# Four more input projections of layer 0 as 512-column products, with an order for minima, copies and sums

## The chip, the cores and the metric

The kernel runs on one core of one Trainium2 chip. The metric is device time in microseconds (us): the median of several executions of the whole program. Before the change it is 244.56 us (three runs, 244.37 to 244.6).

## What is computed

The reference is a decoder trunk of two layers on x of shape 1 x 256 x 1024 (256 positions, model width 1024, all float32). Each layer normalises x, projects it once to 3584 columns, feeds three branches side by side, and projects their gated outputs back:

```
hn   = rms_norm(x, norm_gain)
proj = hn @ w_in                      # 1024 -> 3584 columns
a_q, a_k, a_v, a_g, b_x, b_g, c_q, c_k, c_v, c_g = split(proj)
y_a = dilated_attention(rope(a_q), rope(a_k), a_v) * silu(a_g)   # 8 heads of 64
y_b = rg_lru(b_x) * silu(b_g)                                    # width 256
y_c = stick_breaking(c_q, c_k, c_v) * silu(c_g)                  # 4 heads of 64
x   = x + concat(y_a, y_b, y_c) @ w_out
```

A final `rms_norm` follows the second layer. The dilated attention adds up three windows of dilation 1, 4 and 16 under one softmax. The recurrent branch is a causal convolution of width 4, two sigmoid gates and a linear recurrence h = a h + u. Stick-breaking attention weighs keys by running products of sigmoids.

## The kernel before

**Split products.** Float32 accuracy comes from splitting each operand into a rounded high part (type float32r) and the remainder, the low part, and adding three products: high by high, high by low and low by high. For the activations, `xx` holds both parts side by side: `xh = xx[:, :, 0]`, `xl = xx[:, :, 1]`, eight blocks (k) of 128 features, each 256 positions wide. For the weights, `load_chunk` (L102) brings a chunk of 256 output columns (2048 values on each of 128 partitions) in two transfers of 1024 columns through five staging buffers `st`. For each 512 columns ACT writes the high part (`whi`, L115), and DVE subtracts it from the staged values for the low part (`wlo`, L117). A staging buffer can be loaded again when its two subtractions are done. Chunks are asked for one or two ahead of their use, and four sets of `whi` and `wlo` exist.

**Two forms of projection.** `proj_b` (L326) computes one chunk transposed: 256 output columns in two halves b of 128, each for all 256 positions. The plain form runs 24 products of 256 columns a half (L225, through `mm3`), all three terms into one accumulator; both halves share one PSUM bank, and the reader takes its result from PSUM. The paired form (the chunk is in `PAIRED[l]`) multiplies each high weight block by `xh` and `xl` at once, 512 columns wide (L344, 8 products), and the low weight block by `xh`, 256 wide (L341, 8 products). A half then fills a whole bank: the left 256 columns hold two terms, the right 256 hold high by low. ACT copies the right part into `low` (L347, two buffers) and DVE adds the left part to it (L349). There are three PSUM banks for all projections (pool `pp`), four for scores and transposes (`at`), one for weighted values (`yp`).

**Layer 0 and its scale.** In layer 0 the projections run on x times the gain without the normalisation: the factor 1/rms of each position is multiplied in afterwards, as a row vector `rb` broadcast over partitions. `scaled` (L410) does so in one DVE operation that reads PSUM, `rotated` (L503) does it in the rotation (with a table already multiplied by `rb`) and for the unrotated features (L518). In layer 1, x is normalised first and no factor is needed.

**Order of a layer.** The chunks come in this order: stick-breaking q, k; first dilated q, k (heads 0 to 3); recurrent input (`CH_BX`); second dilated q, k (`CH_AQ[1]`, `CH_AK[1]`, heads 4 to 7); stick-breaking gate (`CH_CG`); recurrent gate (`CH_BG`); two chunks of dilated gate (`CH_AG`, `CH_AG + 1`); four chunks of the output projection (`CH_O` on). Between the two halves of some chunks other work of PE is placed (`mid`): between those of the second q, the scores of heads 0 to 3 (L542), after which DVE takes minima of the masked scores (L549, which also write the shifted scores), ACT the exponentials with their sums (L84), DVE reciprocals and the division (L560, L562). Transposes of these weights (L489) stand between the stick-breaking gate and the recurrent gate; between the halves of the recurrent gate come the gates' products (L601), weighted values (L453) and the scores of heads 4 to 7. After the recurrent gate, `lru_scan` computes the recurrence, and `emit_y` (L437) multiplies it by its gate and splits it into `yh` (L441) and `yl` (L442), which the output projection reads.

**What sets the order.** PE's instructions run in the order in which the program writes them. Those of ACT, DVE and POOL are put in order beforehand by a planner that takes the earliest written instruction that its own estimate of times holds ready; each engine then works through its fixed list and waits where an input or a buffer isn't ready. `dep` (L63) adds an edge to the planner: one instruction comes after another on the same engine's list, without a wait on the chip. Transfers of weights are issued by the SP queue in program order, each when its staging buffer is free.

Layer 0 before pairs only the two chunks of dilated gate, layer 1 all its chunks of `proj_b`.

## Time and profile before

| what | value |
|---|---|
| median of 3 runs | 244.56 us (244.37 to 244.6) |
| profiled execution: its own time, its span | 246.06 us, 244.2 us |
| PE, matmuls busy | 236.2 us (97%), 1651 |
| PE, weight loads busy | 206.6 us (85%), 1651 |
| DVE busy | 200.0 us (82%), 480 |
| ACT busy | 174.4 us (71%), 384 |
| granted TensorE clock | 0.999 |
| DMA | 43.89 MB, mean 180 GB/s |

The span runs from the first to the last instruction on the core; the execution's own time has some 1.9 us around it. PE's busy time counts overlapping products once. The chain of waits follows the work that ended last back to the start; its pieces, in order of time, show where PE runs without a hole. A row of a timeline gives start, length, engine, line, operation, output and inputs, shape and count of neighbours that were merged, and in brackets the idle time of the engine just before and what ended it.

### The profile page before, as it was taken

What the parts mean: (1) busy time and instruction counts of PE and PEld (TensorE: products, weight loads), DVE (VectorE), ACT (ScalarE), POOL (GpSimd) and SP (SyncE); (2) the same over time, 40 slices, a digit from 0 to 9 for tenths busy, and PEclk for the clock granted to TensorE, in tenths of its full rate; (3) what the DMA queues carried; (4) which work ended last, traced back from release to release, by engine and by line L of the source; (5) the groups of instructions that cost most, each with busy time, mean ns of one, the idle gap of its engine ahead of it and who ended that gap; (6) DMA issues with size and microseconds to landing.
All of it is one profiled execution on the core that took longest, in us unless ns stands there. A gap on an engine that the chain in (4) does not pass through costs nothing.

```text
span 244.2 us, 4576 instructions
## 1 busy us (share of the span) xinstructions
PE 236.2 (97%) x1651; PEld 206.6 (85%) x1651; DVE 200.0 (82%) x480; ACT 174.4 (71%) x384; POOL 10.5 (4%) x43
## 2 busy tenths in 40 slices
PE   8799999999999999999999999999999999999991
PEld 4588999999999798878888888888888878887881
DVE  3694699999999889999495585999999986997362
ACT  3677987919597689994673674876669867998143
POOL 0017200002000000000000000000010000000000
PEclk9999999999999999999999999999999999999999
DMA  6989988565846843068448288615470771000022
GB/s 193 377 254 390 384 268 291 190 205 177 240 152 207 272 153 105 1 195 320 175 134 273 88 289 268 199 44 177 171 214 7 226 282 63 31 0 0 3 75 97
DMA packets 14037, 43.89 MB, mean 180 GB/s; under 512 B 1728, under 2 KB 3008, under 8 KB 14016
## 3 DMA queue, kind: packets, MB, share of 16 engines
q1 hardware_dynamic: 13248, 42.43, 51.9%
q0 software_dynamic: 192, 0.52, 0.8%
q10 hardware_dynamic: 576, 0.66, 0.7%
q8 instruction: 13, 0.21, 0.4%
q14 instruction: 8, 0.07, 0.1%
HBM read 42.03 MB, written 1.05 MB: 176 GB/s over the span
## 4 chain that ended last, share of the span: by engine, by line
PE 94%; DMA 3%; DVE 1%; SPq 0%; ACT 0%; issue 0%; DVEq 0%
PE pp L225 34%; PE pp L344 20%; PE pp L341 10%; PE s L225 9%; PE s L181 4%; PE s L489 3%; DMA st<-first 3%; PE y L453 2%; PE pp L383 2%; PE s L542 2%; PE pp L181 2%; PE s L469 1%; PE y L225 1%; PE pp L453 1%; PE s L601 1%; PE s L273 1%
## 5 line engine op out<-in xcount | busy, mean ns | idle before, releaser
L117 DVE TENSOR_TENSOR wlo<-st,whi 128x512 fp32r<-128x512 f32 x128 | 81.8, 684 | 7.5 <-ACT whi L115 6.9
L115 ACT ACTIVATE whi<-st 128x512 fp32r<-128x512 f32 x130 | 72.5, 627 | 9.0 <-DMA st<-w_pack 3.4
L344 PE MATMUL pp<-xx,whi 128*128 128x512 f32 x208 | 50.8, 393 | 0.0
L344 PEld LDWEIGHTS pp<-xx,whi 128*128 128x128 f32 x208 | 37.8, 188 | 7.6 <-DVE q L349 0.3
L225 PE MATMUL pp<-xx,whi 128*128 128x256 f32 x288 | 38.2, 285 | 0.0
L225 PEld LDWEIGHTS pp<-xx,whi 128*128 128x128 f32 x288 | 35.8, 191 | 0.8 <-issue 0.3
L341 PEld LDWEIGHTS pp<-xx,wlo 128*128 128x128 f32 x208 | 26.9, 191 | 1.6 <-ACT scr L84 0.3
L341 PE MATMUL pp<-xx,wlo 128*128 128x256 f32 x208 | 28.0, 284 | 0.0
L225 PE MATMUL pp<-xx,wlo 128*128 128x256 f32 x144 | 20.2, 283 | 0.0
L84 ACT ACTIVATE pr<-scr,mn 128x128 f32<-128x128 f32 (+1 forms) x32 | 14.1, 443 | 6.6 <-DVE mn L549 6.6
L225 PEld LDWEIGHTS pp<-xx,wlo 128*128 128x128 f32 x144 | 18.6, 192 | 0.0
L78 ACT ACT_TABLE_LOAD x13 | 16.7, 1283 | 1.9 <-PEq L847 1.7
L347 ACT ACTIVATE low<-pp 128x256 f32<-128x256 f32 x26 | 9.4, 373 | 8.8 <-PE pp L344 8.0
L225 PE MATMUL pp<-whi,yh 128*128 128x512 f32 (+1 forms) x48 | 14.1, 382 | 0.0
L225 PE MATMUL pp<-wlo,yh 128*128 128x512 f32 (+1 forms) x48 | 13.7, 372 | 0.0
L225 PE MATMUL pp<-whi,yl 128*128 128x512 f32 (+1 forms) x48 | 13.6, 371 | 0.0
L181 PE MATMUL s<-whi,xx 128*128 128x512 f32 (+1 forms) x36 | 9.6, 384 | 1.8 <-ACT xx L161 1.7
L225 PEld LDWEIGHTS pp<-whi,yl 128*128 128x128 f32 x48 | 8.6, 188 | 1.6
L225 PEld LDWEIGHTS pp<-wlo,yh 128*128 128x128 f32 x48 | 8.6, 188 | 1.6
L225 PEld LDWEIGHTS pp<-whi,yh 128*128 128x128 f32 x48 | 8.3, 188 | 1.6 <-issue 0.3
L549 DVE CUSTOM_DVE_ANT_0 scr<-s,con 128x128 f32<-128x128 f32 (+1 forms) x32 | 9.2, 350 | 0.0
L181 PEld LDWEIGHTS s<-whi,xx 128*128 128x128 f32 x36 | 6.0, 197 | 3.3 <-ACT xx L161 2.5
(189 smaller groups left out, 372.3 us busy)
## 6 DMA issues: line engine op xcount, KB each, us to landing
st<-w_pack SPq DMA_DIRECT2D x66, 512.0 KB, 5.3
st<-first SPq DMA_DIRECT2D x7, 512.0 KB, 7.0
xres<-x_in SPq DMA_DIRECT2D x4, 256.0 KB, 7.5
gw_t<-gate_w SPq DMA_DIRECT2D x2, 256.0 KB, 6.8
gn<-gains SPq DMA_DIRECT2D x2, 256.0 KB, 5.9
xs<-xc POOLq DMA_DIRECT2D x4, 128.0 KB, 3.8
gf<-gains SPq DMA_DIRECT2D x2, 256.0 KB, 5.4
out<-st ACTq DMA_DIRECT2D x2, 192.0 KB, 2.0
```

Source lines behind the costliest of these rows:

```text
L78: load = act.preload_act_table_set(name)
L84: i = dep(act.activation(*a, **k), loaded["load"])
L115: split[l, c] = act.activation(h, part, AF.Copy)
L117: dve.tensor_sub(r, part, h.bitcast(F32))
L181: pe.matmul(ps[t][:, c0:c1], a[:, k, t * P:(t + 1) * P], b, start=k == 0 and all(m[0] is not ps for m in seq[:i]), stop=k == NK - 1 and al ...
L225: pe.matmul(ps, a(k), b(k), start=first and i == 0, stop=last and i == len(seq) - 1, skip_group_check=skip)
L341: pe.matmul(ps[:, 0:S], lo[:, k, cs], xh[:, k, :], start=i == 0, stop=i == len(seq) - 1, skip_group_check=True)
L344: pe.matmul(ps, hi[:, k, cs], xx[:, k].rearrange("p h t -> p (h t)"), start=i == 0, stop=i == len(seq) - 1, skip_group_check=True)
L347: act.activation(low, ps[:, S:2 * S], AF.Copy, scale=sc)
L453: pe.matmul(y[hr, p * 128 + o:p * 128 + 256], vt[:, s0, hs], wts[i][s0], start=s0 == 0, stop=s0 == 1)
L489: pe.transpose(tp[:, i * P:(i + 1) * P], tiles[h0 + h][:, j * P:(j + 1) * P], ident)
L549: dve.tensor_tensor_reduce(xs[:, cs], sps[h][:, cs], nmask[:, cs], -0.125, 3e38, ALU.add, ALU.min, mn[:, t:t + 1])
```

## The change

Layer 0 now computes four more chunks in the paired form: the recurrent input, the second dilated q and k, and the stick-breaking gate. The recurrent gate, which sits around the longest piece of other work, stays in the plain form, and so do the first four chunks. For the paired chunks, the factor `rb` is multiplied in after the sums: for the recurrent input in place in the padded input of the convolution, for the gate from its own tile in `silu`, for q and k in the rotation.

The rest is order in layer 0. The four subtractions for the gate's weights come after the last minimum of the scores of heads 0 to 3, and three of them also after the sum of the second half of the second q. The exponentials of the last two of those heads come after that half's copy, and their reciprocals after its sum. The subtractions for the weights of the last dilated gate chunk come after the multiplication of the stick-breaking gate by `rb`. Layer 1's operations are the same as before.

```diff
--- before.py
+++ after.py
@@ -43,7 +43,7 @@
 
 CH_AV, CH_CV, CH_CQ, CH_CK, CH_BX, CH_CG, CH_BG, CH_AG, CH_O = 0, 2, 3, 4, 7, 10, 11, 12, 14
 CH_AQ, CH_AK = (5, 8), (6, 9)
-PAIRED = ((CH_AG, CH_AG + 1), (CH_CQ, CH_CK, CH_AQ[0], CH_AK[0], CH_BX, CH_AQ[1], CH_AK[1], CH_CG, CH_BG, CH_AG, CH_AG + 1))
+PAIRED = ((CH_BX, CH_AQ[1], CH_AK[1], CH_CG, CH_AG, CH_AG + 1), (CH_CQ, CH_CK, CH_AQ[0], CH_AK[0], CH_BX, CH_AQ[1], CH_AK[1], CH_CG, CH_BG, CH_AG, CH_AG + 1))
 
 
 @with_exitstack
@@ -97,7 +97,7 @@
 
     xx, xh, xl = x_tile()
 
-    split, rounds = {}, {}
+    split, rounds, rests = {}, {}, {}
 
     def load_chunk(l, c):
         hi = wsp.tile([P, 2048], F32R, name="whi", tag="whi")
@@ -114,7 +114,7 @@
                     part = v2(part)
                 split[l, c] = act.activation(h, part, AF.Copy)
                 rounds.setdefault((l, c), []).append(split[l, c])
-                dve.tensor_sub(r, part, h.bitcast(F32))
+                rests.setdefault((l, c), []).append(dve.tensor_sub(r, part, h.bitcast(F32)))
         return beside or (hi, lo)
 
     order = [(l, c) for l in range(L) for c in range(NCH) if l > 0 or c > CH_CV]
@@ -344,9 +344,9 @@
                             pe.matmul(ps, hi[:, k, cs], xx[:, k].rearrange("p h t -> p (h t)"), start=i == 0,
                                       stop=i == len(seq) - 1, skip_group_check=True)
                     low = wk.tile([P, S], F32, name="low", tag="low", bufs=2)
-                    act.activation(low, ps[:, S:2 * S], AF.Copy, scale=sc)
+                    last["low"] = act.activation(low, ps[:, S:2 * S], AF.Copy, scale=sc)
                     if sc == 1.0:
-                        dve.tensor_add(to[b], ps[:, 0:S], low)
+                        last["sum"] = dve.tensor_add(to[b], ps[:, 0:S], low)
                     else:
                         dve.scalar_tensor_tensor(to[b], ps[:, 0:S], sc, low, ALU.mult, ALU.add)
                 else:
@@ -358,8 +358,10 @@
             return flat
 
         def proj_to(dst, c, mid=None, sc=1.0):
-            if l > 0 and c in PAIRED[l]:
+            if c in PAIRED[l]:
                 proj_b(c, mid, [dst[:, b, :] for b in range(2)], sc)
+                if l == 0:
+                    dve.tensor_mul(dst, dst, rb.rearrange("p (o t) -> p o t", o=1).broadcast_to([P, 2, S]))
             else:
                 scaled(dst, proj_b(c, mid), sc)
 
@@ -410,7 +412,7 @@
         def scaled(dst, ps, sc=1.0):
             if l == 0:
                 a, b = rows(ps)
-                dve.scalar_tensor_tensor(dst, a, sc, b, ALU.mult, ALU.mult)
+                last["scaled"] = dve.scalar_tensor_tensor(dst, a, sc, b, ALU.mult, ALU.mult)
             else:
                 act.activation(dst, v2(ps), AF.Copy, scale=sc)
 
@@ -425,12 +427,15 @@
         if l > 0:
             tables()
 
+        def home(tile_):
+            return [tile_[:, b, :] for b in range(2)] if l == 0 else None
+
         def silu(dst, ps):
             sg = v2(scr(512))
-            src = v2(ps)
+            src = dst if ps is None else v2(ps)
             if l == 0:
-                src = v2(scr(512))
-                scaled(src, ps)
+                ps, src = src, v2(scr(512))
+                scaled(src, ps.rearrange("p b t -> p (b t)"))
             tab(sg, src, AF.Sigmoid)
             dve.tensor_mul(dst, src, sg)
 
@@ -503,19 +508,20 @@
         def rotated(c, tiles, h0, tag, mid=None):
             dst = tiles[h0] = sb.tile([P, 2, S], F32, name=tag, tag=tag)
             tab_ = rp0 if l == 0 else rp
-            if l > 0:
-                src = scr(S)
-                proj_b(c, mid, [src, dst[:, 1, :]])
+            pair = c in PAIRED[l]
+            if pair:
+                src, high = scr(S), dst[:, 1, :]
+                proj_b(c, mid, [src, high])
             else:
                 ps = proj_b(c, mid)
-                src = ps[:, 0:S]
+                src, high = ps[:, 0:S], ps[:, S:2 * S]
             sh = scr(S)
             dve.stream_shuffle(sh, src, SHUF)
             dve.tensor_mul(dst[:, 0, :], src, tab_[:, 0, :])
             dve.tensor_mul(sh, sh, tab_[:, 1, :])
             dve.tensor_add(dst[:, 0, :], dst[:, 0, :], sh)
             if l == 0:
-                dve.tensor_mul(dst[:, 1, :], ps[:, S:2 * S], rb)
+                dve.tensor_mul(dst[:, 1, :], high, rb)
 
         qT, kT, exact = {}, {}, {}
         prob = {}
@@ -546,18 +552,20 @@
                 xs = scr(384)
                 mn = wk.tile([P, 2], F32, name="mn", tag="mn", bufs=4)
                 for t, cs in halves:
-                    dve.tensor_tensor_reduce(xs[:, cs], sps[h][:, cs], nmask[:, cs], -0.125, 3e38,
-                                             ALU.add, ALU.min, mn[:, t:t + 1])
+                    last["min"] = dve.tensor_tensor_reduce(xs[:, cs], sps[h][:, cs], nmask[:, cs], -0.125, 3e38,
+                                                           ALU.add, ALU.min, mn[:, t:t + 1])
                 shifted[h] = xs, mn
             return shifted
 
         def dil_softmax(shifted):
+            last["exps"], last["recs"] = [], []
             for h, (xs, mn) in shifted.items():
                 pr = wk.tile([P, 384], F32, name="pr", tag="pr", bufs=4)
                 den = wk.tile([P, 2], F32, name="den", tag="den", bufs=4)
                 for t, cs in halves:
-                    tab(pr[:, cs], xs[:, cs], AF.Exp, bias=mn[:, t:t + 1], scale=-1.0, accum_out=den[:, t:t + 1])
-                dve.reciprocal(den, den)
+                    last["exps"].append(tab(pr[:, cs], xs[:, cs], AF.Exp, bias=mn[:, t:t + 1], scale=-1.0,
+                                            accum_out=den[:, t:t + 1]))
+                last["recs"].append(dve.reciprocal(den, den))
                 for t, cs in halves:
                     dve.tensor_scalar(pr[:, cs], pr[:, cs], den[:, t:t + 1], None, ALU.mult)
                 prob[h] = pr
@@ -654,12 +662,20 @@
             dil_softmax(dil_scores(0))
 
         rotated(CH_AQ[1], qT, 4, "q1", second)
+        if l == 0:
+            for r in rests[l, CH_CG]:
+                dep(r, last["min"])
+            for r in last["exps"][4:]:
+                dep(r, last["low"])
+            for r in (*last["recs"][2:], *rests[l, CH_CG][1:]):
+                dep(r, last["sum"])
         rotated(CH_AK[1], kT, 4, "k1")
         split_qk(4, ("q0", "ag"))
         table(SIGM)
-        cg_ps = proj_b(CH_CG)
+        cg_ps = proj_b(CH_CG, None, home(cg))
         pts = dil_transposes(0)
         silu(cg, cg_ps)
+        cg_scaled = last.get("scaled")
 
 
         y_half(0)
@@ -670,7 +686,11 @@
             y_c["y"] = values(va, pts, 0, bank(pp, "pp"))
             y_c["s"] = dil_scores(4)
 
-        silu(bg, proj_b(CH_BG, third))
+        bg_ps = proj_b(CH_BG, third)
+        if l == 0:
+            for r in rests[l, CH_AG + 1]:
+                dep(r, cg_scaled)
+        silu(bg, bg_ps)
         y_half(1)
         table(LN_EXP)
         lru_scan()
```

## The prediction

> **What bounds the kernel now.** I read the page's engine shares and slices first, then the chain of waits in order of time.
>
> ```profile
> span 244.2 us, 4576 instructions
> PE 236.2 (97%) x1651; PEld 206.6 (85%) x1651; DVE 200.0 (82%) x480; ACT 174.4 (71%) x384; POOL 10.5 (4%) x43
> ...
> DVE  3694699999999889999495585999999986997362
> ```
>
> PE is busy for 97% of the span, so every stretch of time that PE gets rid of shortens the kernel, and every wait that it takes on lengthens it. DVE is the engine beside it to watch: from slice 6 to slice 19 (about 31 to 116 us) it is at eight tenths or more throughout. The chain says the same of the stretch in question, and it prices the two kinds of product:
>
> ```profile
> 32.71 5.75 PE pp L225 x48
> ...
> 55.88 2.87 PE pp L225 x24
> 58.75 1.37 PE s L542 x38
> 60.12 14.59 PE pp L225 x120
> 74.71 1.31 PE s L489 x12
> 76.02 2.86 PE pp L225 x24
> ...
> 90.83 3.65 PE pp L344 x16
> ...
> 98.24 2.73 PE s L225 x12
> ...
> 102.29 5.48 PE pp L225 x24
> ...
> 141.27 1.84 PE pp L344 x8
> ...
> 176.29 1.15 PE pp L341 x8
> 177.44 3.65 PE pp L344 x16
> 181.09 1.91 PE pp L341 x16
> 183.01 3.83 PE pp L344 x16
> ```
>
> The rows down to 102.29 are layer 0, the others layer 1 (start, length, what, count). In layer 0 PE goes from one piece to the next without a hole. The 120 products at 60.12 are five halves: second q's other half (to 63.0), second k (to 68.9) and the gate (to 74.7). The last row is one to remember: it is 0.18 us longer than its twin at 177.44.
>
> **The change part by part.** *The products.* A half of an unpaired chunk is 24 products of 256 columns: 5.75 / 48 = 119.8 ns each, 2.875 us a half. A half of a paired chunk is 8 of 512 columns at 3.65 / 16 = 228.1 ns and 8 of 256 at 1.91 / 16 = 119.4 ns, together 1.825 + 0.955 = 2.780 us. So a half gets 0.095 us shorter: the columns are the same 6144, but there are eight instructions fewer. Four chunks (recurrent input, second q, second k, gate) are eight halves: **0.76 us off PE**. After the small score products (L542) the next piece is about 0.2 us long in both forms (14.59 against 5 x 2.875; 1.15 against 0.955), which cancels.
>
> The Trainium skill, "TensorE: Matmul & The Clock Gate", section "Back-to-back issue gap", speaks against this: a warm product takes its columns over 2.4 GHz plus about 2.5 ns. By that a half would go from 24 x 109.2 = 2.62 to 8 x (215.8 + 109.2) = 2.60 us, an estimate of 0.16 us for the eight halves in place of 0.76. The rows above have both widths at a full clock in this kernel, and doubling 119.8 gives 239.6 and not 228.1, so the trace disagrees.
>
> *The evacuations.* Each of the eight halves now needs an ACT copy of its low part and a DVE sum:
>
> ```profile
> L347 ACT ACTIVATE low<-pp x26: 360/372/385, 91.0 to 215.9; 128x256 f32<-128x256 f32 x26
> 98.97 0.64 ACT L347 ACTIVATE low<-pp 128x256 f32<-128x256 f32 x2
> 100.70 0.75 DVE L349 TENSOR_TENSOR scr<-pp,low 128x256 f32<-128x256 f32 x2
> 55.04 0.69 DVE L413 SCALAR_TENSOR_TENSOR bxp<-pp,rb 128x512 f32<-128x512 f32 x1
> 97.72 0.67 DVE L413 SCALAR_TENSOR_TENSOR scr<-agf,rb 128x512 f32<-128x512 f32 x1
> 94.55 0.69 DVE L621 TENSOR_TENSOR it<-it,th 128x512 f32<-128x512 f32 x1
> ```
>
> Back to back, a second ACT copy adds 0.64 - 0.37 = 0.27 us and a second sum 0.75 - 0.42 = 0.33 us: **2.2 us more on ACT and 2.64 us more on DVE**. The multiplication by rb is not new work. For the recurrent input it becomes a plain product of two SBUF tiles (as L621, 0.69) in place of L413 out of PSUM (0.69); for the gate L413 reads an SBUF tile (0.67) in place of PSUM. The rotations read SBUF in place of PSUM, at no difference in these rows.
>
> *Does it fit?* None of this is on PE's chain if it is done in time, so I set DVE's idle time against it:
>
> ```profile
> core 0: us, PE busy (x) PEld busy (x) DVE busy (x) ACT busy (x) POOL busy (x), PEclk, DMA share, GB/s
> 44.90:84.00 39.10, 39.10 (x402) 37.30 (x400) 37.91 (x102) 28.14 (x62) 1.66 (x6) 1.00 0.60 191
> 84.00:98.10 14.10, 14.10 (x93) 12.78 (x90) 13.21 (x42) 11.88 (x30) 0.00 (x0) 1.00 0.43 152
> 98.10:116.00 17.90, 17.90 (x95) 14.51 (x94) 16.84 (x31) 14.26 (x27) 0.00 (x0) 1.00 0.53 177
> 116.00:141.00 25.00, 25.00 (x128) 21.14 (x127) 16.16 (x27) 15.53 (x35) 0.40 (x2) 1.00 0.53 171
> ```
>
> PE wants everything 0.76 us sooner and DVE has 2.64 us more to do, 3.40 us in all. DVE is idle for 39.10 - 37.91 = 1.19 us up to 84, 0.89 up to 98.1, 1.06 up to 116, and 8.84 after that. So **DVE runs late**: by 2.21 us at 84, 1.32 at 98, 0.26 at 116, and then no more. ACT is no bound: 28.14 of 39.10 us plus 2.2.
>
> What runs late is decided by DVE's order. Most of its work up to 84 is the subtractions for weights (L117), which are far ahead of their use:
>
> ```profile
> 59.40 4.29 DVE L117 TENSOR_TENSOR wlo<-st,whi 128x512 fp32r<-128x512 f32 x7
> 63.62 0.28 DVE L549 CUSTOM_DVE_ANT_0 scr<-s,con 128x128 f32<-128x128 f32 x1
> ...
> 75.83 2.49 DVE L117 TENSOR_TENSOR wlo<-st,whi 128x512 fp32r<-128x512 f32 x4
> ...
> SPq L108 <- DVE wlo L117: 49.5, 17, 12.7
> ```
>
> The group at 75.83 belongs to chunk AG+1, whose products begin with the second half of the piece at 90.83, at 92.7, some 14 us after the group ends. The seven at 59.40 (four of the gate, three behind it) end at 63.6; the gate's products start at 68.9 and read them from 68.9 + 1.9. Moved behind the minima (the row at 63.62 is the first of them) and, three of four, behind the sum of second q, which I put at 63.3 below, the gate's subtractions end at 63.3 + 3 x 0.6 = 65.1 (0.6 each by 4.29 / 7) in place of 59.40 + 4 x 0.6 = 61.8, still some 5 us ahead of the first product that reads them. Each pair of subtractions also frees a staging buffer, and the SP queue waits for just that (last row, 49.5 us in 17 waits): those transfers start up to 3 us later, and the 14 us above cover them. I cost the moved subtractions at nothing; with the cover gone they would cost 3 us.
>
> *The order of minima, copies and sums* guards the one new thing that PE waits for: a paired half has a PSUM bank to itself, there are three, so it must be read out within the next two halves, 5.56 us. Layer 1 shows what happens otherwise:
>
> ```profile
> 179.27 0.40 ACT L84 ACTIVATE pr<-scr,mn 128x128 f32<-128x128 f32 x1 [3.93 <-DVE mn L549]
> 182.80 0.36 ACT L347 ACTIVATE low<-pp 128x256 f32<-128x256 f32 x1
> 184.25 0.42 DVE L349 TENSOR_TENSOR q<-pp,low 128x256 f32<-128x256 f32 x1
> 184.72 1.69 PEld L344 LDWEIGHTS pp<-xx,whi 128*128 128x128 f32 x8 [0.30 <-DVE q L349]
> ```
>
> There the second half of second q ends at 179.27 (177.44 + 1.83), its copy stands behind eight exponentials until 182.80, its sum comes at 184.25, and PE waits: the 0.18 us above. In layer 0 the minima now start at 63.62, 3.5 us after their scores end (60.12), so without the order the wait would be no smaller. With it, minima start near 60.1, four exponentials (eight take 182.80 - 179.27 = 3.53 us) end near 62.5, and that half ends at about 62.4 (63.0 less its share of the gain): copy near 62.8, sum near 63.3, needed at 68. That is 4 us of cover. Bounds for what PE still loses on banks: 0, and 0.18 for each of the four chunks, 0.72. I take 0.1, nearer to nothing, since the order removes just this case.
>
> **Sum.** 0.76 - 0.1 = 0.66 us less. The profiled execution took 246.06 us (span 244.2 and 1.9 around it) and would go to 245.4; the median of the runs is 244.56, so I predict **243.9**. About 0.2%, 0.49 us, is what a measurement of this kernel can tell from no change: from 244.07 down it counts as faster, from 245.05 up as slower.
>
> **The rivals.** *No change that shows.* Either layer 1's wait comes back at three or four chunks (0.54 to 0.72 of the 0.76 gone), or DVE is late where it matters. The nearest place is the recurrence's output:
>
> ```profile
> 87.12 0.69 DVE L413 SCALAR_TENSOR_TENSOR scr<-pp,rb 128x512 f32<-128x512 f32 x1 [0.38 <-PE pp L225]
> 87.73 1.28 DVE L117 TENSOR_TENSOR wlo<-st,whi 128x512 fp32r<-128x512 f32 x2
> ...
> 98.77 0.68 DVE L442 TENSOR_TENSOR yl<-scr,yh 128x512 fp32r<-128x512 f32 x1
> ...
> 100.34 0.63 PE L225 MATMUL s<-whi,yl 128*128 128x512 f32 x2
> ```
>
> L442 ends at 99.45 and PE reads it at 100.34: 0.89 us to spare. If DVE is late there by the 1.32 us worked out above, PE waits 0.43 and the gain is 0.33: 244.2. For it: DVE's queue is one fixed order. Against: the subtractions at 87.73 and after belong to the second output chunk, which PE reads from the middle of the piece at 102.29 on, and they can fall behind instead. That a wide product saves nothing (the page's rule) ends here too, at 244.4; the rows speak against it.
>
> *Slower.* DVE's lateness of 2.21 us at 84 falls whole on the chain that starts at 87.12, the gate of the recurrence, through scan and L442: PE then waits 2.21 - 0.89 = 1.32 us in the output projection, the balance is 0.56 us worse, 245.1. It decides from 0.89 + 0.76 = 1.65 us of lateness on. For it: the added sums stand ahead of subtractions that are forced behind them, and these may be put in front of L413. Against: L413 now waits for PE (0.38 idle), and the stretch from 84 to 98.1 has 0.89 us of idle time that takes lateness up.
>
> **How the numbers follow.** Forecast 0.57, with its own range 243.75 (0.76 and nothing lost, less a little scatter) to 244.07. No change 0.28, of which 0.04 for width that saves nothing. Slower 0.15. The range 243.6 to 245.0 takes in both bounds of the bank waits and of the lateness up to the slower case. Faster 0.57, same 0.28, slower 0.15.
>
> **What would show it.** In layer 0's chain between 48 and 76 us, pieces of L344 x16 near 3.65 and L341 x16 near 1.91 show the price; pieces longer than that show bank waits, and the weight loads' waits name L349 or L347. Minima near 60 and the copy of second q's second half ahead of the fifth exponential show the order. The first reading of yh and yl by the output projection, now 98.24 in the chain, should come near 97.5 (PE's whole gain), and the next layer's first paired piece, now 141.27, near 140.6. A hole in PE between 98 and 101 us makes the slower rival right; a gain well beyond 0.8 us would mean that I have missed a cost of PE.

## The result: slower by 0.9%, and the profile after

The changed kernel takes 247.14 us (median of 6 executions, 246.31 to 247.98) against 244.58 us of the kernel before on the same chip (6 executions, 244.37 to 245.53). The ratio is 1.009 with a 95% interval of 1.0069 to 1.0111: about 2.2 us slower, where 0.66 us faster was forecast. The time lies outside the range of 243.6 to 245.0. The profiled execution took 247.98 us.

The page of the changed kernel, span and engine shares:

```profile
span 246.1 us, 4458 instructions
PE 236.9 (96%) x1587; PEld 203.9 (83%) x1587; DVE 202.6 (82%) x488; ACT 177.0 (72%) x392; POOL 10.8 (4%) x43
```

DVE has grown by the 2.6 us that the sums were to cost (200.0 to 202.6), ACT by 2.6 us. PE's busy time has not fallen, and the share is no longer 97%: PE waits. Where it waits is read from the start of five pieces that every version of this kernel has: the scores of stick-breaking, the scores of heads 0 to 3, the transposes, the scores of heads 4 to 7, and the first products of the output projection. PE's timeline of before, then of after (start, length, line, operation, count, and in brackets a wait and its releaser):

```profile
38.39 1.58 PE L469 MATMUL s<-kc,qc 64*128 64x128 f32 x16
58.68 0.73 PE L542 MATMUL s<-k,q 32*128 32x128 f32 x16
74.54 1.48 PE L489 MATMUL s<-con,pr 128*128 128x128 f32 x12
82.59 0.73 PE L542 MATMUL s<-k,q 32*128 32x128 f32 x16
98.08 0.62 PE L225 MATMUL s<-whi,yh 128*128 128x512 f32 x2
```

```profile
37.57 1.58 PE L474 MATMUL s<-kc,qc 64*128 64x128 f32 x16
57.60 0.73 PE L548 MATMUL s<-k,q 32*128 32x128 f32 x16
71.41 1.22 PE L341 MATMUL pp<-xx,wlo 128*128 128x256 f32 x8 [1.05 <-DVE scr L349]
74.30 1.48 PE L494 MATMUL s<-con,pr 128*128 128x128 f32 x12
82.36 1.14 PE L548 MATMUL s<-k,q 32*128 32x128 f32 x14
93.83 2.11 PE L344 MATMUL pp<-xx,whi 128*128 128x512 f32 x8 [0.76 <-DVE agf L349]
99.54 0.61 PE L225 MATMUL s<-whi,yh 128*128 128x512 f32 x2
```

The first row starts at 38.39 in the one execution and at 37.57 in the other, and between 36.31 and 38.44 over all runs here, so I compare distances between the rows and not times. Stretch A (first row to the second scores) went from 20.29 to 20.03. Stretch B (to the transposes) went from 15.86 to 16.70, C (to the scores of heads 4 to 7) from 8.05 to 8.06, D (to the output projection) from 15.49 to 17.18. From there to layer 1's stick-breaking scores (stretch OS) both take 57.05 us, and from those scores to the last row of PE's timeline it is 83.3 us in every version. The sum over the five stretches is 2.28 us more than before, which is what the ratio says.

So A gained what three halves should gain (0.26 of 3 x 0.095 = 0.29). B, with five halves, should have come to about 15.4 (15.86 less 5 x 0.095) and lost **1.30 us**; D lost **1.69 us**. The waits of PE's weight loads between 40 and 104 us account for B's loss and for 1.5 us of D's (waiting engine, what for, total, times, longest):

```profile
PEld pp L341 <- DVE scr L349: 1.3, 1, 1.3
PEld pp L344 <- DVE agf L349: 1.2, 1, 1.2
PEld s L548 <- ACT it L84: 0.3, 1, 0.3
```

All three are waits for a PSUM bank to be read out. By the starts of PE's pieces, D's loss is 0.62 us at the scores of heads 4 to 7 (1.98 us from their start to the next piece, 1.36 before) and some 1.0 us at the dilated gate. The chain of waits of after tells what stood ahead of each reading:

```profile
71.02 0.35 DVE scr L349
71.41 1.22 PE pp L341 x8
...
93.44 0.34 DVE agf L349
93.83 2.11 PE pp L344 x8
...
99.70 2.73 PE s L225 x12
...
142.73 1.84 PE pp L344 x8
```

Before, this part of the chain was PE throughout. Now it runs over DVE between 39 and 93 us but for some 5 us of PE and ACT. The output projection's first piece stands at 99.70, where 97.5 was forecast, and layer 1's first paired piece at 142.73 instead of 140.6. Since this execution is 0.82 us ahead of the one before at the first row, both pieces are some 3 us later than forecast.

**The first wait.** DVE's and then ACT's timeline of after:

```profile
64.01 0.42 DVE L349 TENSOR_TENSOR q<-pp,low 128x256 f32<-128x256 f32 x1
...
68.19 0.68 DVE L117 TENSOR_TENSOR wlo<-st,whi 128x512 fp32r<-128x512 f32 x1
...
69.13 1.88 DVE L117 TENSOR_TENSOR wlo<-st,whi 128x512 fp32r<-128x512 f32 x3
70.94 0.41 DVE L349 TENSOR_TENSOR scr<-pp,low 128x256 f32<-128x256 f32 x1
...
76.50 0.69 DVE L534 TENSOR_TENSOR qk<-k,qk 128x512 fp32r<-128x512 f32 x1 [1.60 <-ACT qk L533]
...
89.15 0.68 DVE L415 SCALAR_TENSOR_TENSOR scr<-pp,rb 128x512 f32<-128x512 f32 x1
...
93.36 0.42 DVE L349 TENSOR_TENSOR agf<-pp,low 128x256 f32<-128x256 f32 x1
```

```profile
62.25 0.36 ACT L347 ACTIVATE low<-pp 128x256 f32<-128x256 f32 x1
...
65.68 0.38 ACT L347 ACTIVATE low<-pp 128x256 f32<-128x256 f32 x1
...
75.31 0.63 ACT L115 ACTIVATE whi<-st 128x512 fp32r<-128x512 f32 x1 [2.15 <-DMA st<-w_pack]
...
89.86 0.63 ACT L84 ACTIVATE scr<-scr 128x512 f32<-128x512 f32 x1 [1.11 <-DVE scr L415]
90.52 1.28 ACT L78 ACT_TABLE_LOAD   x1
91.81 0.91 ACT L84 ACTIVATE av<-rt,c 128x256 f32<-128x256 f32 x2
92.62 0.36 ACT L347 ACTIVATE low<-pp 128x256 f32<-128x256 f32 x1
```

The first half of the *second k* is copied at 65.68, but its sum starts at 70.94, five microseconds later. Four subtractions for the recurrent gate's weights (68.19 and 69.13), which PE reads only behind the transposes at 74.30, stand ahead of it. The second half of the gate's chunk wants that bank.

**The second wait.** The scaling of the recurrent gate (L415) starts at 89.15, ACT's sigmoid waits for it (89.86), behind the sigmoid ACT loads a table (90.52) and computes the recurrence's exponentials (91.81), and behind those stands the copy of the dilated gate's first half (92.62); its sum at 93.36 releases the bank for the next chunk. Two more things are visible here. DVE idles for 1.60 us at 76.50, for ACT; and ACT waits at 75.31 for a transfer. The waits of ACT for weights' transfers between 44 and 98 us, before and then after:

```profile
ACT whi L115 <- DMA st<-w_pack: 0.5, 1, 0.5
```

```profile
ACT whi L115 <- DMA st<-w_pack: 4.4, 3, 2.2
```

This gives three suspects: the new banks (pairs), the order that holds subtractions back (through staging buffers, transfers and ACT's queue), and DVE's load.

### The profile page after: what moved, and what is told of

Read it like the earlier page. It is cut to its first block, busy times and chain, and to the rows that moved or that the text cites. A ratio compares the mean times of both kernels' runs of the same rounds, so it can differ in the third digit from the quotient of the medians.

```text
span 246.1 us, 4458 instructions
## 1 busy us (share of the span) xinstructions
PE 236.9 (96%) x1587; PEld 203.9 (83%) x1587; DVE 202.6 (82%) x488; ACT 177.0 (72%) x392; POOL 10.8 (4%) x43
## 4 chain that ended last, share of the span: by engine, by line
PE 73%; DVE 21%; DMA 2%; ACT 1%; issue 1%; SPq 0%; DVEq 0%
PE pp L344 19%; PE pp L225 18%; PE pp L341 10%; PE s L225 9%; DVE wlo L117 8%; PE s L181 4%; PE s L494 3%; DMA st<-first 2%; PE pp L385 2%; PE pp L181 2%; PE y L458 2%; DVE scr L555 2%; DVE sw L485 1%; PE y L225 1%; PE s L548 1%; PE s L474 1%
## 5 line engine op out<-in xcount | busy, mean ns | idle before, releaser
L344 PE MATMUL pp<-xx,whi 128*128 128x512 f32 x272 | 66.8, 393 | 0.8 <-DVE agf L349 0.8
L344 PEld LDWEIGHTS pp<-xx,whi 128*128 128x128 f32 x272 | 49.3, 188 | 10.8 <-DVE agf L349 1.4
L225 PE MATMUL pp<-xx,whi 128*128 128x256 f32 x160 | 21.1, 285 | 0.0
L225 PEld LDWEIGHTS pp<-xx,whi 128*128 128x128 f32 x160 | 19.9, 191 | 0.5 <-issue 0.3
L347 ACT ACTIVATE low<-pp 128x256 f32<-128x256 f32 x34 | 12.4, 374 | 10.4 <-PE pp L344 9.6
L181 PE MATMUL s<-whi,xx 128*128 128x512 f32 (+1 forms) x36 | 10.1, 402 | 0.5 <-ACT xx L161 0.4
L485 DVE TENSOR_TENSOR_SCAN sw<-scr,con 128x127 f32<-128x127 f32 (+1 forms) x16 | 8.0, 538 | 1.0 <-ACT scr L84 1.0
```

The costliest lines, as they stand in the source:

```text
L181: pe.matmul(ps[t][:, c0:c1], a[:, k, t * P:(t + 1) * P], b, start=k == 0 and all(m[0] is not ps for m in seq[:i]), stop=k == NK - 1 and al ...
L225: pe.matmul(ps, a(k), b(k), start=first and i == 0, stop=last and i == len(seq) - 1, skip_group_check=skip)
L344: pe.matmul(ps, hi[:, k, cs], xx[:, k].rearrange("p h t -> p (h t)"), start=i == 0, stop=i == len(seq) - 1, skip_group_check=True)
L347: last["low"] = act.activation(low, ps[:, S:2 * S], AF.Copy, scale=sc)
L485: dve.tensor_tensor_scan(w[:, lo:lo + n][:, ::-1], om[:, lo + 1:lo + 1 + n][:, ::-1], diag[:, 255 - n:255][:, ::-1], 0.0, ALU.mult, ALU.add)
```

## The experiments

Each run's table row gives the five stretches of its profiled execution, worked out as above, their sum against before's, and the ratio to the kernel before on the same chip with its 95% interval. "a" and "b" are the kernels after and before that the edit starts from.

| run | A | B | C | D | OS | sum | ratio |
|---|---|---|---|---|---|---|---|
| before | 20.29 | 15.86 | 8.05 | 15.49 | 57.05 | | |
| after | 20.03 | 16.70 | 8.06 | 17.18 | 57.05 | +2.28 | 1.009 [1.0069, 1.0111] |
| after_again (a) | 20.03 | 16.72 | 8.06 | 17.32 | 57.05 | +2.44 | 1.012 [1.0095, 1.0144] |
| pairs_no_order (a) | 20.03 | 16.91 | 8.06 | 16.44 | 57.05 | +1.75 | 1.0063 [1.0041, 1.0085] |
| order_no_pairs (a) | 20.29 | 15.86 | 8.05 | 16.90 | 57.05 | +1.41 | 1.0036 [1.0014, 1.0057] |
| min_order_only (a) | 20.29 | 15.86 | 8.05 | 16.38 | 57.05 | +0.89 | 1.0033 [1.0011, 1.0055] |
| k_sums_first (a) | 20.03 | 15.40 | 8.06 | 16.80 | 57.05 | +0.60 | 1.0045 [1.0014, 1.0077] |
| k_first_no_ag (a) | 20.03 | 15.40 | 8.06 | 17.16 | 57.05 | +0.96 | 1.0047 [1.0029, 1.0065] |
| sums_only (a) | 20.03 | 15.40 | 8.06 | 17.54 | 57.05 | +1.34 | 1.006 [1.0038, 1.0082] |
| fewer_subs (a) | 20.03 | 16.73 | 8.06 | 16.00 | 57.05 | +1.13 | 1.0048 [1.0031, 1.0065] |
| pool_subs (a) | 20.03 | 15.84 | 8.88 | 17.76 | 57.05 | +2.82 | 1.0143 [1.0118, 1.0168] |
| delay_bg (b) | 20.29 | 15.86 | 8.05 | 16.26 | 57.05 | +0.77 | 1.0038 [1.0017, 1.006] |
| bx_cg (a) | 20.12 | 15.70 | 8.06 | 16.47 | 57.05 | +0.66 | 1.0029 [1.0009, 1.0048] |
| sums_early_gate (a) | 20.03 | 15.40 | 8.06 | 15.49 | 58.62 | +0.86 | 1.0036 [1.0019, 1.0053] |
| early_fewer (a) | 20.03 | 15.40 | 8.06 | 15.49 | 58.73 | +0.97 | 1.0052 [1.0033, 1.0072] |
| tuned_order (a) | 20.03 | 15.40 | 8.06 | 15.49 | 57.57 | -0.19 | 0.9983 [0.9962, 1.0003] |
| tuned_norm (a) | 20.03 | 15.40 | 8.53 | 15.53 | 57.02 | -0.23 | 0.9999 [0.9983, 1.0015] |
| before_norm (b) | 20.29 | 15.86 | 8.05 | 15.70 | 57.05 | +0.21 | 1.001 [0.9999, 1.0022] |
| two_norm (a) | 20.03 | 15.40 | 8.06 | 15.72 | 57.05 | -0.48 | 0.9979 [0.9958, 0.9999] |
| tail_first (a) | 20.03 | 15.40 | 8.06 | 15.49 | 57.05 | -0.71 | 0.9977 [0.9957, 0.9998] |

### Pairs and order apart

**pairs_no_order** takes both blocks of edges out of after; **order_no_pairs** takes the pairs out and keeps the two edges that need no pairs: the gate's subtractions behind the last minimum, those of the last dilated gate chunk behind the gate's scaling.

```diff
 # pairs_no_order
-        if l == 0:
-            for r in rests[l, CH_CG]:
-                dep(r, last["min"])
-            for r in last["exps"][4:]:
-                dep(r, last["low"])
-            for r in (*last["recs"][2:], *rests[l, CH_CG][1:]):
-                dep(r, last["sum"])
...
-        if l == 0:
-            for r in rests[l, CH_AG + 1]:
-                dep(r, cg_scaled)
 # order_no_pairs
-PAIRED = ((CH_BX, CH_AQ[1], CH_AK[1], CH_CG, CH_AG, CH_AG + 1),
+PAIRED = ((CH_AG, CH_AG + 1),
...
-            for r in last["exps"][4:]:
-                dep(r, last["low"])
-            for r in (*last["recs"][2:], *rests[l, CH_CG][1:]):
-                dep(r, last["sum"])
```

> The four chunks are paired, none of the new order edges is there. Late sums (DVE has 2.64 us too much to do, and what PE waits for stands behind subtractions for weights): as slow as the change or slower, 247 to 248.5 us, with a first PE wait before 71 us, since the sum of second q now comes behind all eight exponentials. Order edges to blame (they push the gate's subtractions back, staging buffers come free late, ACT stands waiting for a transfer and DVE behind it): 244 to 245 us, and ACT waits for transfers under 1.5 us between 55 and 80 us (5.5 us in the changed kernel).

> The kernel before with the two edges that need no pairs: the gate's four subtractions behind the last minimum, those of the last dilated gate chunk behind the gate's scaling. Late sums: no change that shows, 244.3 to 245.0 us, PE without a wait over 0.3 us in layer 0. Order edges to blame: 245.5 to 247 us.

Each half of the change loses alone: the pairs 1.75 us in the trace, the edges 1.41 us, without a single new product or sum. The pairs without order lose 1.51 us in B (waits of 1.0 us at second q's sum and 0.5 at second k's) and 0.95 in D. The edges without pairs lose only in D. Their waits between 44 and 98 us:

```profile
ACT whi L115 <- DMA st<-w_pack: 6.2, 4, 2.1
...
DVE cg L440 <- ACT scr L84: 2.1, 1, 2.1
```

The gate's four subtractions, held behind the minima, keep their staging buffers; the SP queue issues the next four transfers at 64.96, 67.09, 69.97 and 71.17, where before has them at 60.7, 61.92, 63.12 and 66.70, though its first row comes 0.63 us later; ACT, whose list is fixed, stands 6.2 us waiting for them, and whatever is behind in its list is late: the sigmoid of the gate, for which DVE then idles 2.1 us. **min_order_only**, of both edges the first alone, and a repetition of after:

```diff
 # min_order_only: order_no_pairs, and
-            for r in rests[l, CH_AG + 1]:
-                dep(r, cg_scaled)
```

> The kernel before with one edge: the stick-breaking gate's four subtractions come behind the last minimum; nothing is paired. If it is this edge that makes transfers late (staging buffers free 4 to 7 us later, ACT waits for transfers 6.2 us with both edges, and the gate's sigmoid, the recurrence's sigmoids and all behind them stand in ACT's queue): 0.8 to 1.6 us slower than before, ACT waiting for transfers over 4 us between 44 and 98 us. If the other edge (last dilated gate chunk behind the gate's scaling) is to blame: within 0.3 us of before.

> The changed kernel itself, beside the kernel before on the chip of the runs that it is compared with: 1.8 to 2.6 us slower than before by every theory.

The first edge costs 0.89 of the 1.41 us, again in D alone. The repetition of after gives the same waits within 0.15 us.

### The bank of second k

```diff
 # k_sums_first: after, and
         rotated(CH_AK[1], kT, 4, "k1")
+        if l == 0:
+            for r in rests[l, CH_BG]:
+                dep(r, last["sum0"])
 # k_first_no_ag: k_sums_first without the edge on rests[l, CH_AG + 1]
```

> The changed kernel with one edge more: the recurrent gate's four subtractions come behind the first sum of second k. Late sums: the wait of 1.1 to 1.3 us at 71 us is gone, but DVE's load is the same and its lateness shows further on, at the scores of heads 4 to 7 and at the first sum of the dilated gate: 245.8 to 247.1 us. Order edges to blame: another subtraction pushed back, no gain or a loss, 247 to 248 us.

> The changed kernel with the recurrent gate's subtractions behind the first sum of second k, and without the edge that holds the last dilated gate chunk's subtractions behind the gate's scaling. If that edge is to blame for the loss between the scores of heads 4 to 7 and the output projection (1.3 us with it): that loss falls to 0.9 us or less, and the whole is within 0.5 us of before. If the edge behind the minima is to blame, or DVE's load: no gain over the kernel with the edge, 0.8 to 1.5 us slower than before.

One edge that puts the recurrent gate's four subtractions behind the first sum of second k takes B's loss away whole: 16.70 to 15.40, which is 0.46 us under before, 0.092 for each of the five halves. DVE's timeline of k_sums_first shows the order turned round:

```profile
68.57 0.42 DVE L349 TENSOR_TENSOR scr<-pp,low 128x256 f32<-128x256 f32 x1
...
69.24 2.49 DVE L117 TENSOR_TENSOR wlo<-st,whi 128x512 fp32r<-128x512 f32 x4
```

B is settled by this. D's loss stays, with or without the edge on the last gate chunk (16.80 and 17.16). This edge takes 0.36 us off D here, and adds 0.52 in the kernel without the pairs (16.38 and 16.90): its cost depends on what else is in the list.

### D: held-back subtractions, or DVE's load?

```diff
 # sums_only: k_sums_first, and
-            for r in rests[l, CH_CG]:
-                dep(r, last["min"])
-            for r in (*last["recs"][2:], *rests[l, CH_CG][1:]):
+            for r in last["recs"][2:]:
                 dep(r, last["sum"])
-            for r in rests[l, CH_AG + 1]:
-                dep(r, cg_scaled)
 # fewer_subs: after, and in load_chunk
+                if (l, c) == (0, CH_AG):
+                    lo = ready[l, CH_BG][1]
+                    continue
 # bx_cg: after without edges, and
-PAIRED = ((CH_BX, CH_AQ[1], CH_AK[1], CH_CG, CH_AG, CH_AG + 1),
+PAIRED = ((CH_BX, CH_CG, CH_AG, CH_AG + 1),
```

> All four chunks paired, with the edges that put copies and sums ahead (exponentials 5 to 8 behind the copy of second q, their reciprocals behind its sum, the recurrent gate's subtractions behind the first sum of second k), and without both edges that hold back the gates' subtractions. If bank waits at second q and k are the loss there: the stretch from the scores of heads 0 to 3 to the transposes takes 15.4 us (15.86 before, 16.91 without any edge). After that DVE's load is the same, so the later stretch stays at 16.2 to 17.2 against 15.49: 0.0 to 1.0 us slower than before. If holding back the subtractions was the only cause of the later loss: 15.5 to 15.9, and 0.3 to 0.7 us faster.

> The changed kernel without the four subtractions for the first dilated gate chunk of layer 0 (its low parts are left out, and the recurrent gate's low parts are multiplied in their place, so the values are not the reference's). DVE has 2.4 us less to do up to 84 us, which takes back nearly all of the sums' 2.64 us. Late sums: the wait at 71 us stays or shrinks little (the subtractions in front of it are others), the waits at 83 and 93 us go: 245.2 to 246 us. Order edges to blame: 246.5 to 247.2 us.

> Only the recurrent input and the stick-breaking gate paired, no new edges: 0.38 us less on PE, 1.3 us more on DVE, which idles 1.19 us between 44.9 and 84 us in the kernel before. If DVE's load counts from its idle time on: the later stretch loses 0.3 us or less, and the whole is 0.1 to 0.4 us faster than before, not told from no change. If any added sum in front of the recurrent gate's scaling is lost one for one: the later stretch 16.4 or more, 0.4 to 1.0 us slower.

sums_only takes out both of the change's edges that hold gates' subtractions back; the recurrent gate's four stay behind the first sum of second k. ACT now waits for transfers 0.6 us instead of 4.4, and D is no better, 17.54. So the held-back subtractions lose time in D by themselves (order_no_pairs), but they aren't the only cause, and the runs give no share for them in the changed kernel: there D is 17.18 with all edges and 16.44 with none, while next to the cure for second k it is 16.80 with them and 17.54 without. With four subtractions fewer on DVE (2.4 us; fewer_subs) D falls from 17.18 to 16.00. With half the new sums (bx_cg, 1.3 us on DVE, no edges) D still loses 0.98, and here all of it stands at the banks of the scores of heads 4 to 7: from their start at 82.19 to the next piece at 84.53 it takes PE 2.34 us, 1.36 in before, and the wait named there is for ACT's sigmoid. PE's timeline of bx_cg:

```profile
83.18 0.50 PE L548 MATMUL s<-k,q 32*128 32x128 f32 x8 [0.25 <-ACT it L84]
```

The scaling of the recurrent gate comes 0.48 us after the dilated gate's first product and costs nothing. So what DVE has ahead of this stretch matters (fewer_subs), and the loss comes through two banks. Whether bx_cg loses by its sums on DVE or by its copies on ACT isn't separated.

**delay_bg** tests the second of them by itself, in the kernel before: two products on DVE that nobody reads, between the last minimum and the scaling of the recurrent gate.

```diff
 # delay_bg: before, and
-        silu(bg, proj_b(CH_BG, third))
+        bg_ps = proj_b(CH_BG, third)
+        if l == 0:
+            late = [dep(dve.tensor_mul(rp0, rp, rp), last["min"]) for _ in range(2)]
+        silu(bg, bg_ps)
+        if l == 0:
+            for i in late:
+                dep(last["scaled"], i)
```

> The kernel before with two products of 128x512 on DVE that nobody reads (0.6 us each) between the last minimum of heads 4 to 7 and the scaling of the recurrent gate. If the chain scaling, sigmoid, table load, exponentials, ACT copy of the dilated gate's first half, its DVE sum, PSUM bank has no slack in the kernel before: PE waits about 0.9 us more at that bank (1.2 less the 0.34 us between the sum's end at 92.16 and the product at 92.50), the stretch from the scores of heads 4 to 7 to the output projection goes from 15.49 to 16.3 or more, 0.8 to 1.2 us slower than before. If the nearest place is the recurrence's low parts with 0.89 us of slack, as in the prediction: 0.3 us lost, 15.8, no change that shows.

The scaling starts 1.55 us after the first product of the dilated gate, where it is 0.20 us in before and 1.83 us in after, and D grows by 0.77 us. PE's timeline of delay_bg has the same wait as after's, at the same place:

```profile
91.07 2.11 PE L344 MATMUL pp<-xx,whi 128*128 128x512 f32 x8 [0.48 <-DVE agf L349]
```

Here is how near that place is in the kernel before. DVE's and PE's timelines of before:

```profile
91.74 0.42 DVE L349 TENSOR_TENSOR agf<-pp,low 128x256 f32<-128x256 f32 x1
```

```profile
90.67 2.68 PE L344 MATMUL pp<-xx,whi 128*128 128x512 f32 x11
```

The sum ends at 92.16; the ninth of the products that begin at 90.67, the first into that bank, is due 8 x 0.228 us later, at 92.49. That is **0.33 us of slack** at the sum. The scaling has more, as ACT's timeline of before shows:

```profile
86.16 2.20 ACT L115 ACTIVATE whi<-st 128x512 fp32r<-128x512 f32 x4 [2.36 <-PE pp L225]
88.26 0.61 ACT L84 ACTIVATE scr<-scr 128x512 f32<-128x512 f32 x1
```

The scaling ends at 87.81, but the sigmoid stands behind four roundings of weights until 88.26. From the scaling's start to the sum's start it is 4.62 us in before, and 4.21 in delay_bg and in after, where the sigmoid waits for the scaling (4.21 or 4.22 in every run that loses at this bank). So the scaling has 0.41 + 0.33 = **0.74 us** to spare. delay_bg delayed it by 1.55 - 0.20 = 1.35 us, 0.61 more than that, and the product into the bank starts 0.66 us late (91.07, due at 90.41); the other 0.11 of the 0.77 us is lost behind it. For after, with 1.63 us of delay, the same sum gives 0.89, and its product starts 0.94 us late (93.83, due at 92.89). So this bank's loss in after goes back to the late scaling nearly whole.

### Undoing the loss

**sums_early_gate** orders the rest of the recurrence's chain: the roundings of the first output chunk behind the hyperbolic tangents, its subtractions behind the scaling of the recurrent gate, the exponentials of the recurrence behind the copy of the dilated gate's first half, the second output chunk's subtractions behind that gate's sum. **early_fewer** is the same with the four subtractions of fewer_subs left out.

```diff
 # sums_early_gate: sums_only, and
+                for r in rounds[l, CH_O]:
+                    dep(r, last["th"])
+                for r in rests[l, CH_O]:
+                    dep(r, bg_scaled)
+                for b in range(2):
+                    dep(last["av", b], last["low0"])
+            for r in rests[l, CH_O + 1]:
+                dep(r, ag_sum)
```

> The kernel with sums first and, in the later stretch, four more edges: the first output chunk's high copies behind the recurrence's sigmoids, its subtractions behind the scaling of the recurrent gate, the recurrence's exponentials behind the ACT copy of the dilated gate's first half, and the second output chunk's subtractions behind that half's sum. If the loss there is what stands in front of the gates' sigmoids and of that first sum: 15.5 to 16.0 in the later stretch, 0.2 to 0.7 us faster than before. If it is DVE's load as such: the wait moves to the recurrence's high and low parts in the output projection, 16.2 or more, no faster than before.

> The kernel with sums first and the gate early, without the four subtractions for the first dilated gate chunk of layer 0 (its low parts are left out, the recurrent gate's are multiplied in their place, so the values are not the reference's). DVE's load as such: the output projection's stretch, 58.62 there, comes back to 57.05 to 57.4, and the whole is 0.3 to 0.8 us faster than before. Order alone: 58 us or more, no faster than before.

D is back at 15.49 with all of DVE's new work still there. So D's loss was a matter of what stands ahead of what; which of the four edges brings how much wasn't separated. The loss comes back behind the output projection's start (58.62), where PE now waits for the recurrence's output:

```profile
PEld s L225 <- ACT yh L447: 1.0, 1, 1.0
PEld pp L225 <- DVE scr L445: 0.6, 1, 0.6
```

Taking 2.4 us of work off DVE does not help there (58.73): this is order as well, the output chunks' subtractions between the steps of the recurrence.

```diff
 # tuned_order: sums_early_gate, and
             for r in rests[l, CH_O + 1]:
-                dep(r, ag_sum)
+                dep(r, last["yl", 2])
 # tuned_norm: tuned_order, and for heads 0 to 3; two_norm: for heads 0 and 1; before_norm: before, heads 0 to 3
-    dve.tensor_scalar(pr[:, cs], pr[:, cs], den[:, t:t + 1], None, ALU.mult)
+    act.activation(pr[:, cs], pr[:, cs], AF.Copy, scale=den[:, t:t + 1])
 # tail_first: tuned_order, and behind the residual additions of the first 128 positions (c: layer 1's first chunk)
-                dve.tensor_add(xres[:, t, cs], o_ps[t, n2], xres[:, t, cs])
+                done = dve.tensor_add(xres[:, t, cs], o_ps[t, n2], xres[:, t, cs])
+                if (l, t) == (0, 0):
...
+                            for r in rests[1, c][2:]:
+                                dep(r, done)
```

> The same kernel with all its work, the second output chunk's subtractions behind the recurrence's low parts in place of behind the dilated gate's first sum: 2.4 us less in front of those low parts. Order alone: the output projection's stretch comes back to 57.05 to 57.4 and the whole is 0.3 to 0.8 us faster than before. DVE's load as such: PE waits in the output projection or behind it for 0.5 us or more, the whole is within 0.4 us of before or slower.

> As tuned_order, and the division of heads 0 to 3 in layer 0 (eight products, 1.8 us on DVE) is done by ACT copies with a scale, 2.5 to 3 us more there. By either theory PE's stretches take 20.03, 15.40, 8.06, 15.5 and 57.1 us, and the whole is 0.4 to 0.8 us faster than before, unless ACT now stands in front of the gates' sigmoids.

> The kernel before with heads 0 to 3 of layer 0 divided on ACT. Its PE does not wait there, so by either theory no change that shows, within 0.3 us.

> tuned_order with the division of heads 0 and 1 alone on ACT (four operations instead of eight). Theory that DVE's load sets the last stretch: 57.05 or 57.02, as with all four heads; theory that ACT's queue is full from 70 to 78 us: the stretch from the transposes to the scores of heads 4 to 7 loses half of what it lost with four heads, 0.24 of 0.47 us. Together 0.3 to 0.7 us less than before, ratio 0.997 to 0.999.

> tuned_order with one more edge: the last two subtractions for layer 1's first chunk stand behind the two residual additions of the first 128 positions, not ahead of them. In tuned_order they start at 115.53 after 0.91 us of waiting for a transfer, and the additions follow at 116.74, when the weights of PE's last output products are long done. If that is what the stretch from the output projection to layer 1 still loses (57.57 against 57.05), it comes back to 57.05 with the three stretches before it at 15.40, 8.06 and 15.49: 0.26 + 0.46 = 0.72 us less than before, ratio 0.9971. If the products' gain is worth nothing in the end, the ratio stays within 0.2% of 1.

tuned_order leaves 0.52 us in OS. Moving the division of four heads to ACT takes that away and loses 0.48 in C, where ACT's copies of the transposes come later; in the kernel before the same move costs 0.21. With two heads C is untouched and D loses 0.23, which I had under neither theory. The cleaner cure is tail_first: the last two subtractions for layer 1's first chunk, whose high part ACT rounds late because it waits for a transfer, had stood ahead of the residual additions. With this one edge more all five stretches are at before's (within 0.01) or under it, **0.71 us less in the trace, ratio 0.9977 with an interval of 0.9957 to 0.9998**: faster than the kernel before and so than the changed one (1.009), though the interval ends close to 1. Its chain of waits is PE without a hole from 57 us to the output projection:

```profile
58.18 1.15 PE pp L341 x8
59.33 3.65 PE pp L344 x16
62.98 1.91 PE pp L341 x16
```

These are the prediction's prices to the hundredth: 3.65 and 1.91 us for two halves, in layer 0.

### Subtractions on POOL

```diff
 # pool_subs: k_sums_first, and the four subtractions of the first dilated gate chunk
-                dve.tensor_sub(r, part, h.bitcast(F32))
+                gps.tensor_sub(r, part, h.bitcast(F32))
```

> The changed kernel with the recurrent gate's subtractions behind the first sum of second k, and the first dilated gate chunk's four subtractions in layer 0 on POOL, which is idle then. DVE has 2.4 us less to do. If DVE's load is what is left of the loss: the stretch from the scores of heads 4 to 7 to the output projection shortens by 0.6 us or more against 16.8, and the whole comes to within 0.5 us of before. If late transfers and ACT's queue are the cause, or if POOL slows DVE down: no gain, 0.8 to 1.5 us slower than before.

The slowest run of all, for a reason of its own. POOL's and DVE's timelines of pool_subs:

```profile
67.16 4.61 POOL L117 TENSOR_TENSOR wlo<-st,whi 128x512 fp32r<-128x512 f32 x3 [5.67 <-ACT whi L115]
```

```profile
68.03 1.17 DVE L525 TENSOR_TENSOR q<-q,rb 128x256 f32<-128x256 f32 x1
69.12 1.52 DVE L522 TENSOR_TENSOR scr<-scr,rp 128x256 f32<-128x256 f32 x1
70.56 0.41 DVE L349 TENSOR_TENSOR scr<-pp,low 128x256 f32<-128x256 f32 x1
70.89 1.16 DVE L523 TENSOR_TENSOR q<-q,scr 128x256 f32<-128x256 f32 x1
71.98 3.58 DVE L117 TENSOR_TENSOR wlo<-st,whi 128x512 fp32r<-128x512 f32 x4
```

POOL takes 1.46 us for a subtraction, DVE 0.68. While POOL subtracts, a product of two SBUF tiles takes DVE 1.17, 1.52 and 1.16 us, where the same product takes 0.41 and 0.42 in k_sums_first, and four subtractions take 3.58 us instead of 2.49. The sum, with one operand in PSUM, takes its usual 0.41. These rows are 0.76 + 1.10 + 0.74 + 1.09 = 3.7 us longer, more than the 2.4 us that left DVE, and what stands behind them is later (B 15.84 against 15.40 in k_sums_first, C 8.88, D 17.76). That the longer rows cause these losses is read from the rows. Late transfers don't explain them: ACT waits 2.1 us for transfers between 44 and 98 us, 2.8 in k_sums_first.

## Why the prediction was wrong, point by point

**The products: right.** "0.76 us off PE": k_sums_first has 0.26 in A and 0.46 in B, 0.72 together, and tail_first brings 0.71 of it to the end. The Trainium skill's gap rule ("TensorE: Matmul & The Clock Gate", section "Back-to-back issue gap") gave an estimate of 0.16. That section gives its formula for a single isolated product and puts a sustained stream at some 131 ns for 512 columns; the rows of 3.65 us for 16 such products in layer 0, 228 ns each, disagree with both.

**The evacuations: right in size.** DVE's two sums back to back stand 0.33 us apart (70.94 and the next at 71.27 in after), and DVE's whole busy time grew by 2.6 us.

**"I cost the moved subtractions at nothing": wrong, the first step that failed.** The cover of 5 and 14 us was counted to the product that reads the weights. What came due first was the staging buffer. I named that link, SP waiting for subtractions, and let the same 14 us cover it; but a late transfer stops ACT at its rounding, and everything behind it in ACT's list, long before PE wants the weights. order_no_pairs measures this step alone: 1.41 us in the trace, within the 3 us that I gave for "cover gone". What the step costs inside the whole change isn't shown.

**"I take 0.1" for the banks, bounds 0 to 0.72: wrong, the second.** I worked out one bank, that of second q's second half, and it was no trouble: its copy is at 62.25, ahead of the last exponentials, and its sum at 64.01. The forecast was 62.8 and 63.3, which is 62.0 and 62.5 on the clock of this execution; 64.01 is still some 3 us ahead of the next use. The bounds came from layer 1, where a late sum had cost 0.18. Second k's first half wasn't worked out; subtractions that nothing held back stood before its sum, and it cost 1.30 us by itself, k_sums_first shows.

**The lateness of DVE: right that it comes, wrong where it bites, the third.** I let the idle time of DVE take up lateness over a whole window, and took the reader with 0.89 us to spare (L442) as the nearest. The nearest was the bank of the dilated gate's first half, with 0.33 us at its sum and 0.74 at the scaling of the recurrent gate, on which it hangs through ACT: a sigmoid, a table load, two exponentials and a copy. A second bank, that of the scores of heads 4 to 7, cost 0.62 us and wasn't in the prediction at all. The prediction's own rival "slower" starts on the same instruction, the scaling at 87.12, but followed it through the scan to L442, wanted 1.65 us of lateness before it decides, and gave 245.1, just above the stated range. In after that scaling is 1.63 us later against PE than before; the bank behind it loses 1.07 of the 1.69 us of D. That rival had a chance of 0.15 and was the right kind of story: its slack was near the real one, its end too distant. What the forecast had wrong is the idle time that was to take the lateness up. In before it is nearly all waiting for other engines (0.46 and 0.70 us for ACT of the 1.19 up to 84 us), and in after DVE waits 1.60 us for ACT at 76.50 alone.

**What is shown and what is argued.** Shown by an edit: B's loss (k_sums_first), the cost of the edges alone (order_no_pairs, min_order_only), the bank behind the scaling (delay_bg), that order without any work taken away restores the gain (tail_first, with eight groups of edges at once). Argued from rows only: how D's 1.69 us in after, 0.62 at the scores' bank and 1.07 at the dilated gate's by PE's starts, splits by cause into held-back transfers, the scores' bank and DVE's load; the three overlap, and sums_only shows that taking away one leaves the others.

## What to carry to other kernels

When a change adds evacuations, list every bank that they hold and, for each, what stands ahead of its reader on that engine's list; one bank examined says nothing of the next. A moved instruction is not free because its result is needed late: ask what buffer it holds, which transfer waits for that buffer and which in-order engine stops at that transfer. Measure slack at the nearest reader of the whole chain, through the other engines, before setting idle time of an engine against lateness.

## What the runs showed of the hardware that I had not expected

That POOL might slow DVE was one answer expected of pool_subs; how much, and that it goes by the kind of operand, was not: 1.17 and 1.52 us for a product of two SBUF tiles of 128x256 beside POOL's subtraction, 0.41 us for a sum with one operand in PSUM. The lengths fit a block better than a share: POOL's three subtractions end near 68.7, 70.2 and 71.8 (an estimate: 4.61 us by three, from 67.16), and DVE's slow products end at 69.20, 70.64 and 72.05, which is 0.5, 0.4 and 0.3 us behind, about one duration of their own. The Trainium skill, "SBUF — State Buffer", section "Who interferes with whom", says that a DVE instruction with two SBUF inputs contends with a GpSimd instruction that reads SBUF, that one with at most one SBUF input does not (outside modes that no row here shows), and that the port pair they share is an exclusive lock; the trace agrees, with 0.41 us beside POOL's subtraction for the one and 1.16 to 1.52 for the other.
